# Loads of the stored projection weights begun from ScalarE's queue instead of SyncE's

## The chip, the cores and the metric

One core of one Trainium2 chip runs the whole program. The metric is the device time of one execution in microseconds (us). The core's engines each have an instruction stream of their own, run in order: TensorE (PE, with its weight loads as PEld), VectorE (DVE), ScalarE (ACT), GpSimd (POOL) and SyncE (SP). A transfer between HBM and on-chip memory is begun by an instruction in the stream of one of them; 16 DMA engines then move it.

## The reference

One inference step of a backbone with one layer: 128 context tokens and 2,048 latent tokens of width 1,024. Cut to what matters here:

```
h    = rmsnorm(x) * (1 + scale) + shift              # per token
proj = h @ w_in                                      # 1,024 -> 3,088 columns
u, z_s5, qkv, z_gdn, beta, a = split(proj)
s5   = gelu(S5 scans of u, both directions) * sigmoid(z_s5)
gdn  = gated DeltaNet of silu(conv3(qkv)), both directions, gated by silu(z_gdn)
x    = x + gate * (concat(s5, gdn) @ w_out)
x    = x + gate * (relu(rmsnorm(x)... @ w_mlp_in)^2 @ w_mlp_out)
out  = rmsnorm(x), and the final S5 and DeltaNet states of the context
```

Matrix products are made in three passes, since each float32 operand is split into a high and a low part: high by high, low by high, high by low.

## The kernel before

**Stages.** Time in the program falls into three stretches. Up to about 410 us the kernel normalises the tokens, makes tables, and projects the first group of tokens. From 410 to about 1424 us it projects the other groups, and beside that runs the S5 scans (lines 1265 to 1375), the DeltaNet preparation (lines 587 to 829) and the DeltaNet steps (lines 869 to 990). From 1424 us on it makes the output projection and the MLP (lines 1448, 1534 and 1556).

**The projection.** `group_proj` (line 471) walks over column tiles `ct` of 128 columns of `w_in`. For each it gets two weight tiles of 128 x 8 x 128 floats (512 KB each), the high part `wh` and the low part `wl`, and runs 24 matmuls a block of tokens on line 482: eight with `wh` on the high part of the tokens `hH`, eight with `wl` on `hH`, eight with `wh` on the low part `hL`. The sums stand in a PSUM bank `d`, of which there are three and, in the later groups, two. `evac` (line 490) empties the bank: for the qkv columns ScalarE (line 502), VectorE (504, 506), ScalarE (508), VectorE (510), then a store from SyncE (514); for the z columns lines 495 to 498 and 517 to 521.

**The weights.** The first time a column tile is needed, `load_w` (line 392) loads it raw, splits it and stores both parts in HBM in `s_wc` (line 398); 20 tiles are stored so. Each later time it loads the two stored parts back (line 403). This happens 68 times, so there are 136 such loads, 71 MB in all. The pool `pw` has two buffers for `wh` and two for `wl`: a load can begin when the last matmul that reads the tile of two column tiles before has run.

**What sets the order.** The program is written as generators that take turns, and a scheduler then puts the instructions of every engine into one fixed order by a timeline of its own. Each DMA raises one of eight completion semaphores, DMAHW0 to DMAHW7, that are given out in turn; before a DMA begins, its engine waits until the DMA that held the same semaphore before has landed. In the kernel before all DMAs of the program are begun by SyncE, so a load on line 403 stands in one stream with the stores of lines 514, 521, 720 and 756 and with the other loads, among them the tokens `hH` and `hL` (line 387).

Of the kernel before, what the change touches and what calls it, by code (L numbers as in the profile page):

```python
# [8 lines left out]
F32 = mybir.dt.float32  # L9
# [382 lines left out]
def load_w(k, ct):  # L392

    nc = k.nc
    if ct not in k.wdone:
        wh, wl = split_w(k, k.I['w_in'][0][:, ct * 128:ct * 128 + 128])
        for i, w in enumerate((wh, wl)):
            nc.sync.dma_start(k.S['wc'][ct, i], w.bitcast(F32).rearrange("p k c->p (k c)"))
        k.wdone.add(ct)
        return wh, wl  # L400
    ws = [k.pw.tile([128, 8, 128], FR, name=n) for n in ("wh", "wl")]
    for i, w in enumerate(ws):
        nc.sync.dma_start(w.bitcast(F32).rearrange("p k c->p (k c)"), k.S['wc'][ct, i])
    return ws


def split_w(k, src, p=None, nm=""):
    nc = k.nc
    p = p or k.pw
    wh = p.tile([128, 8, 128], FR, name="wh" + nm)  # L410
    wl = p.tile([128, 8, 128], FR, name="wl" + nm, bufs=1 if nm else k.wlb)
    w = k.pwr.tile([128, 8, 128], F32, name="wraw")
    nc.sync.dma_start(w, src.rearrange("(k p) c->p k c", p=128))
    nc.scalar.activation(wh, w, AF.Copy)
    nc.gpsimd.tensor_tensor(wl, w, wh.bitcast(F32), op=OP.subtract)
    return wh, wl
# [54 lines left out]
def group_proj(k, gi, cts):  # L471
    nc, I = k.nc, k.I
    H, L, blocks, off = k.cur
    for ct in cts:
        wh, wl = load_w(k, ct)
        for (f, w, span, segs) in blocks:
            ps = k.psd.tile([128, 512], F32, name="d")
            n = 0

            for (W_, X_) in ((wh, H), (wl, H), (wh, L)):  # L480
                for kk in range(8):
                    nc.tensor.matmul(ps[:, 0:w], W_[:, kk, :], X_[kk][:, f:f + w], start=(n == 0), stop=(n == 23))  # L482
                    n += 1
            evac(k, ct, ps, span, segs, off)
        if ct == 23:
            k.zg |= {c for (f, w, span, segs) in blocks for (o, m, tk) in segs for c in range(tk // 128, (tk + m + 127) // 128)}
        yield None
# [1420 lines left out]
```

## Time and profile before

| | |
|---|---|
| Three timed runs | 3278.9, 3288.34, 3278.14 us; median 3278.9 us |
| The profiled execution | 3283.95 us, its span 3282.2 us |
| Busy in the span | PE 3018.0, PEld 2554.5, DVE 1986.4, ACT 1113.0, POOL 1351.0 us |
| Mean granted TensorE clock | 0.946 |
| DMA | 594.98 MB, mean 181 GB/s |

A busy time is the time in which an engine had at least one instruction at work; the rest of the span it waited for another engine, for a transfer or for nothing that the profile shows. Instructions that begin a DMA are not counted as busy. They are marked with a q behind the engine's name (SPq). The granted clock is the share of TensorE's full speed: 1.0 stands for 2.4 GHz, 0.5 for 1.2 GHz.

### The profile page before, as it was taken

To read this page: it belongs to the slowest core of one execution; us is meant where nothing else is said; L and a number is where in the kernel's file an instruction comes from. 1 tells how busy PE (TensorE), PEld (TensorE's weight loads), DVE (VectorE), ACT (ScalarE), POOL (GpSimd) and SP (SyncE) were. 2 spreads that over 40 slices of the span, in tenths; PEclk is the share of its full clock that TensorE was granted. 3 is DMA by queue.
4 is the path that set the end of the run, shared out by engine and by line. 5 is a ranking of instruction groups with operands and counts; after the bars stand their busy time and mean duration, and the time that the engine had idled before them with its cause. 6 is when DMAs were issued, how large, how long until landed. Compare 5 with 4: busy or idle time off the path is not lost. (4 is left out here: it accounts for less than half of the span.)

```text
span 3282.2 us, 48952 instructions
## 1 busy us (share of the span) xinstructions
PE 3018.0 (92%) x17978; PEld 2554.5 (78%) x17978; DVE 1986.4 (61%) x3842; ACT 1113.0 (34%) x2338; POOL 1351.0 (41%) x983
## 2 busy tenths in 40 slices
PE   5899989889887889988999999999999999999998
PEld 2778967677776677877888778898888887888886
DVE  6635579777776886346545368543358643684445
ACT  2334334424433222234423243322233322433332
POOL 3532223413444332246543454333444544554542
PEclk7889989898988899989999999999999999999999
DMA  7789888966567888899533455322444534553332
GB/s 208 174 178 223 237 292 259 303 220 205 176 223 228 259 277 287 299 301 321 163 95 112 150 164 167 103 77 75 134 123 143 156 97 125 164 170 100 97 96 71
DMA packets 572752, 594.98 MB, mean 181 GB/s; under 512 B 167228, under 2 KB 428592, under 8 KB 569440
## 3 DMA queue, kind: packets, MB, share of 16 engines
q1 hardware_dynamic: 572512, 591.86, 58.9%
q8 instruction: 141, 2.31, 0.3%
q14 instruction: 99, 0.81, 0.1%
HBM read 449.61 MB, written 142.13 MB: 180 GB/s over the span
## 5 line engine op out<-in xcount | busy, mean ns | idle before, releaser
L1411 POOL TENSOR_TENSOR wol<-woraw,woh 128x512 fp32r<-128x512 f32 x320 | 426.7, 1345 | 648.4 <-ACT woh L1410 637.2
L1410 ACT ACTIVATE woh<-woraw 128x512 fp32r<-128x512 f32 x320 | 193.4, 626 | 802.8 <-PE gA L1556 470.8
L1561 DVE TENSOR_TENSOR acc<-acc,gA 128x512 f32<-128x512 f32 x510 | 341.0, 682 | 192.5 <-PE gA L1556 192.4
L1556 PE MATMUL gA<-woh,ffH 128*128 128x512 f32 x1088 | 426.0, 392 | 6.8 <-ACT r L1538 3.9
L1556 PE MATMUL gA<-woh,ffL 128*128 128x512 f32 x1088 | 425.5, 391 | 1.8 <-DVE ffL L1542 1.8
L1556 PE MATMUL gA<-wol,ffH 128*128 128x512 f32 x1088 | 425.0, 391 | 0.0
L1411 POOL TENSOR_TENSOR wil<-wiraw,wih 128x1024 fp32r<-128x1024 f32 x128 | 328.6, 2569 | 112.0 <-PE gA L1534 84.7
L1541 DVE TENSOR_TENSOR r<-r 128x512 f32<-128x512 f32 (+1 forms) x160 | 163.9, 1031 | 304.7 <-ACT ffH L1540 304.4
L1534 PE MATMUL gA<-htH,wih 128*128 128x512 f32 (+1 forms) x1280 | 276.6, 362 | 5.8 <-DVE acc L1561 3.3
L1534 PE MATMUL gA<-htL,wih 128*128 128x512 f32 (+1 forms) x1280 | 272.8, 358 | 0.0
L1534 PE MATMUL gA<-htH,wil 128*128 128x512 f32 (+1 forms) x1280 | 271.9, 357 | 0.0
L1534 PEld LDWEIGHTS gA<-htH,wih 128*128 128x128 f32 x1280 | 222.8, 190 | 39.1 <-DVE acc L1561 5.0
L1534 PEld LDWEIGHTS gA<-htL,wih 128*128 128x128 f32 x1280 | 221.5, 188 | 30.6
L1556 PEld LDWEIGHTS gA<-woh,ffH 128*128 128x128 f32 x1088 | 205.4, 189 | 51.2 <-ACT r L1538 4.8
L1534 PEld LDWEIGHTS gA<-htH,wil 128*128 128x128 f32 x1280 | 220.5, 188 | 29.8
L1556 PEld LDWEIGHTS gA<-woh,ffL 128*128 128x128 f32 x1088 | 205.3, 189 | 44.0 <-DVE ffL L1542 2.2
L1556 PEld LDWEIGHTS gA<-wol,ffH 128*128 128x128 f32 x1088 | 205.3, 189 | 43.0
L482 PE MATMUL d<-hH,wh 128*128 128x258 f32 (+2 forms) x960 | 178.8, 329 | 23.1 <-DMA wh<-s_wc 18.2
L482 PE MATMUL d<-hL,wh 128*128 128x258 f32 (+2 forms) x960 | 177.8, 319 | 9.5 <-DMA hL<-s_hL 9.4
L482 PEld LDWEIGHTS d<-hH,wh 128*128 128x128 f32 x960 | 150.8, 209 | 40.6 <-issue 24.2
L482 PE MATMUL d<-hH,wl 128*128 128x258 f32 (+2 forms) x960 | 176.0, 320 | 0.0
L1410 ACT ACTIVATE wih<-wiraw 128x1024 fp32r<-128x1024 f32 x128 | 134.7, 1052 | 121.1 <-PE gA L1534 80.7
(419 smaller groups left out, 5603.0 us busy)
## 6 DMA issues: line engine op xcount, KB each, us to landing
wiraw<-in_w_mlp_in SPq DMA_DIRECT2D x128, 512.0 KB
woraw<-in_w_mlp_out SPq DMA_DIRECT2D x256, 256.0 KB
wh<-s_wc SPq DMA_DIRECT2D x68, 512.0 KB
wl<-s_wc SPq DMA_DIRECT2D x68, 512.0 KB
wada<-in_w_ada SPq DMA_DIRECT2D x24, 1024.0 KB
KVr<-s_kv SPq DMA_DIRECT2D x34, 512.0 KB
Qr<-s_qkv SPq DMA_DIRECT2D x32, 512.0 KB
woraw<-in_w_out SPq DMA_DIRECT2D x64, 256.0 KB
```

What stands on the lines that cost most here:

```text
L482: nc.tensor.matmul(ps[:, 0:w], W_[:, kk, :], X_[kk][:, f:f + w], start=(n == 0), stop=(n == 23))
L1410: nc.scalar.activation(h[:, i:i + n], w, AF.Copy)
L1411: sub.tensor_tensor(l[:, i:i + n], w, h[:, i:i + n].bitcast(F32), op=OP.subtract)
L1534: nc.tensor.matmul(ps[b][:, 0:w], W[:, kk, :], X[:, kk, b * w:b * w + w], start=(m == 0), stop=(m == 23))
L1541: nc.vector.tensor_tensor(r[:, 0:w], r[:, 0:w], r[:, 0:w], op=OP.mult)
L1556: nc.tensor.matmul(ps, X[:, s], W[:, hf], start=(m == 0), stop=(m == 3 * FB - 1))
L1561: nc.vector.tensor_tensor(accs[i][:, c], accs[i][:, c], ps, op=OP.add)
```

## The change

One word in `load_w`: the two DMAs that load a stored column tile are begun from ScalarE's instruction stream.

```diff
@@ load_w, line 403
     ws = [k.pw.tile([128, 8, 128], FR, name=n) for n in ("wh", "wl")]
     for i, w in enumerate(ws):
-        nc.sync.dma_start(w.bitcast(F32).rearrange("p k c->p (k c)"), k.S['wc'][ct, i])
+        nc.scalar.dma_start(w.bitcast(F32).rearrange("p k c->p (k c)"), k.S['wc'][ct, i])
     return ws
```

The scheduler puts all streams into a new order. Without the waits, ScalarE's stream goes from 2,153 to 2,289 instructions and SyncE's from 1,956 to 1,820; TensorE's keeps its 15,585, of which the first 2,156 and the last 6,485 stand as before and those between are mixed differently. Two places follow, with the waits in brackets: a wait on an engine's name is for work of that engine, one on a DMAHW name for a transfer. The number behind a tile's name is that of its buffer.

SyncE before, around the loads of one column tile (`wh_8310`, `wl_8311`) in the second group of tokens; `s_qkv` and `s_rw` are stores to HBM of projected columns and of DeltaNet factors:

```order
L514 DMA s_qkv_70<-ec3_7956 128x2x128 [waits DMAHW2_49,DVE_49]
L756 DMA s_rw_73<-W_5966 4x16x1024 [waits DVE_49]
L756 DMA s_rw_73<-W_5966 4x16x1024
L514 DMA s_qkv_70<-ec3_7992 128x2x128 [waits DMAHW5_49,DVE_49]
L756 DMA s_rw_73<-UB_6312 4x16x1024 [waits DMAHW6_49,Activation_49]
L756 DMA s_rw_73<-UB_6312 4x16x1024 [waits DMAHW7_49]
L514 DMA s_qkv_70<-ec3_8082 128x2x128 [waits DMAHW0_49,DVE_49]
L403 DMA wh_8310<-s_wc_61 128x1024 [waits DMAHW1_49,PE_49]
L403 DMA wl_8311<-s_wc_61 128x1024 [waits DMAHW2_49]
```

ScalarE with the change, at the same loads; lines 502 and 508 are the evacuation of the blocks of the tile before, line 753 a DeltaNet copy:

```order
L403 DMA wh_8153<-s_wc_61 128x1024 [waits DMAHW5_49,DMAHW1_49]
L508 ACTIVATE ec2_7990<-ec1_7988 128x256 [waits DVE_49,Activation_49]
L502 ACTIVATE ec1_8074<-d_8049,cw_152 128x256 [waits PE_49,Activation_49]
L403 DMA wl_8311<-s_wc_61 128x1024 [waits DMAHW4_49,PE_49]
L508 ACTIVATE ec2_8080<-ec1_8078 128x256 [waits DVE_49,Activation_49]
L753 ACTIVATE UB_6312<-W_5966 128x1024 [waits DVE_49]
L502 ACTIVATE ec1_8110<-d_8085,cw_152 128x256 [waits PE_49,Activation_49]
L403 DMA wh_8310<-s_wc_61 128x1024 [waits DMAHW6_49,DMAHW3_49]
L508 ACTIVATE ec2_8116<-ec1_8114 128x256 [waits DVE_49,Activation_49]
```

The two loads have left the row of stores, and each now stands between two evacuations: `wl` ahead of the first step of a block's evacuation, `wh` behind it.

The second place is among the z columns, where DeltaNet steps (lines 934 and 955) run beside the projection. SyncE with the change, around the stores of the inverse (`s_inv`, line 829):

```order
L886 DMA Qr_13800<-s_qkv_70 128x1024 [waits DMAHW7_49,PE_49]
L829 DMA s_inv_76<-R0_12720 128x512 [waits DMAHW0_49,DVE_49]
L829 DMA s_inv_76<-R0_12720 128x512 [waits DMAHW1_49]
L829 DMA s_inv_76<-R1_12721 128x512 [waits DMAHW2_49,DVE_49]
L829 DMA s_inv_76<-R1_12721 128x512 [waits DMAHW3_49]
L887 DMA Rr_13802<-s_inv_76 128x512 [waits DMAHW4_49,PE_49]
L883 DMA KVr_13801<-s_kv_75 128x1024 [waits DMAHW5_49,PE_49,Pool_49]
```

and ScalarE with the change, at the load whose semaphore is DMAHW2, the same as that of the first store of `R1_12721` above:

```order
L955 ACTIVATE o_13749<-p4_13750,gsc_94 128x128 x3
L934 ACTIVATE w_13741<-p1_13736 128x512 [waits PE_49]
L403 DMA wl_14437<-s_wc_61 128x1024 [waits DMAHW2_49,DMAHW1_49,PE_49]
L517 ACTIVATE ec2_14297<-d_14272 128x512 [waits DVE_49,PE_49,Activation_49]
L403 DMA wh_14436<-s_wc_61 128x1024 [waits DMAHW6_49,DMAHW4_49]
L955 ACTIVATE o_13833<-p4_13834,gsc_94 128x128 [waits DMAHW6_49]
```

In the kernel before, the load `wl_14437` stood in SyncE's stream 22 DMAs ahead of the first of these stores; now the stores come first, and ScalarE waits for one of them to land before it begins the load and evacuates `d_14272`.

## Rows read from the trace of the kernel before

**Rows 1.** Stretches: busy us of PE, PEld, DVE, ACT, POOL; clock, DMA share, GB/s
```profile
410.00:1424.00 1014.00, 881.14 (x6971) 745.38 (x6968) 742.67 (x1925) 345.19 (x964) 333.17 (x298) 0.91 0.78 253
1424.00:3282.00 1858.00, 1791.76 (x8642) 1520.93 (x8640) 1017.43 (x1383) 616.74 (x1093) 870.64 (x553) 0.98 0.45 137
...
700.00:710.00 10.00, 2.90 (x13) 2.94 (x14) 5.86 (x28) 1.20 (x3) 0.71 (x2) 0.65 0.72 256
710.00:720.00 10.00, 10.00 (x94) 9.64 (x93) 5.46 (x19) 1.88 (x6) 2.42 (x2) 0.84 0.50 143
```

**Rows 2.** Line 403: its instructions (duration ns min/median/max, first and last start us)
```profile
L403 SPq DMA_DIRECT2D wh<-s_wc x68: 319/377/2693, 409.9 to 1414.5; - x68
L403 SPq DMA_DIRECT2D wl<-s_wc x68: 319/389/1875, 410.5 to 1412.3; - x68
```

**Rows 3.** What PE waited for, 410 to 1424 us (us in total, times, longest)
```profile
PE gs L1367 <- DVE S L1355: 23.3, 6, 7.3
PE d L482 <- DMA wh<-s_wc: 18.2, 10, 7.7
PE gT L660 <- ACT kv L650: 10.6, 3, 4.8
...
PE d L482 <- DMA hL<-s_hL: 9.4, 4, 7.5
...
PE g L786 <- DMA RW<-s_rw: 7.2, 1, 7.2
...
PE p L927 <- DMA Qr<-s_qkv: 4.6, 1, 4.6
PE p L937 <- ACT w L934: 4.2, 5, 1.3
```

**Rows 4.** What SP's queue waited for, 410 to 1424 us
```profile
SPq L403 <- PE d L482: 39.5, 34, 5.6
...
SPq L403 <- DMA hH<-s_hH: 2.3, 3, 1.2
```

**Rows 5.** SP in order of time, 688 to 710 us (start, duration)
```profile
690.88 2.08 SPq L514 DMA_DIRECT2D s_qkv<-ec  x1
693.06 2.95 SPq L756 DMA_DIRECT2D s_rw<-UB  x2
696.10 0.86 SPq L514 DMA_DIRECT2D s_qkv<-ec  x1
697.05 1.22 SPq L403 DMA_DIRECT2D wh<-s_wc  x1
```

**Rows 6.** PE in order of time, 688 to 712 us
```profile
689.89 1.11 PE L482 MATMUL d<-hL,wh 128*128 128x258 f32 x8
...
693.01 1.20 PE L482 MATMUL d<-hH,wh 128*128 128x258 f32 x8 [1.55 <-DMA wh<-s_wc]
...
707.10 3.78 PE L482 MATMUL d<-hH,wh 128*128 128x258 f32 x16 [7.71 <-DMA wh<-s_wc]
```

**Rows 7.** ACT in order of time, 676 to 710 us
```profile
692.15 0.46 ACT L502 ACTIVATE ec<-d,cw 128x256 f32<-128x256 f32 x1
```

**Rows 8.** What DVE waited for, 410 to 1424 us
```profile
DVE ga L1371 <- ACT ga L1370: 30.7, 15, 11.7
DVE ec L504 <- ACT ec L502: 22.5, 10, 4.5
DVE ec L496 <- ACT ec L495: 19.0, 8, 5.5
DVE R L803 <- ACT TA L802: 17.8, 9, 4.8
```

**Rows 9.** What ACT waited for, 410 to 1424 us
```profile
ACT U L740 <- DMA UB<-s_ub: 16.5, 4, 8.0
```

**Rows 10.** ACT in order of time, 1195 to 1203 us
```profile
1199.34 0.60 ACT L934 ACTIVATE w<-p 128x512 f32<-128x512 f32 x1 [4.16 <-PE p L932]
```

**Rows 11.** SP in order of time, 1194 to 1242 us
```profile
1235.32 2.08 SPq L829 DMA_DIRECT2D s_inv<-R  x4
```

## The prediction

> **What bounds the kernel now.** I read the stretches first. The loads that the change moves stand between 409.9 and 1414.5 us [rows 2], so the stretch from 410 to 1424 us is the one that it touches. There TensorE is busy 881.14 of 1014 us, VectorE 742.67, ScalarE 345.19, the DMA engines 0.78 of the time, and TensorE is granted 0.91 of its clock; behind it, TensorE is busy 1791.76 of 1858 us at 0.98 [rows 1]. The last stretch is TensorE's own work, which the change leaves as it is. The projection stretch has no single bound: TensorE lacks 1014 - 881 = 133 us in it, and only this idle time, and the clock that goes down behind it, can be won or lost.
>
> Next the waits of TensorE in that stretch. The longest entry, 23.3 us, is for VectorE in the S5 scan. The moved loads come second: matmuls waited 18.2 us in ten places for a `wh` tile, 7.7 of them in one. Other transfers, all begun by SyncE, cost 9.4 (`hL`), 7.2 (`RW`) and 4.6 us (`Qr`), together 21.2 [rows 3].
>
> Last, the orders of time around that longest wait. TensorE finished the last matmuls with an older `wh` at 689.89 + 1.11 = 691.00 us, and at 707.10 us it still waited for the tile that went into this buffer [rows 6]. SyncE had begun that load at 697.05 us only: from 690.88 us on it was at a store of line 514, two of line 756 and another of line 514 [rows 5]. The load was late because of what stood ahead of it in its stream, not only because of its transfer.
>
> **The change, part by part.** Sums are made against the profiled execution, 3283.95 us; its span is 3282.2 us, and the median of the three runs is 3278.9, 5.05 us less.
>
> *The loads' place.* In the new order the load at 697.05 us stands on ScalarE directly behind the line 502 that ended at 692.15 + 0.46 = 692.61 us [rows 7]. That is 4.44 us earlier, or 57% of the 7.71 us that TensorE waited. I take 57% of the 18.2 us: **-10.4 us**. The bounds are 0, if the transfers get no quicker by an earlier start, and -18.2.
>
> *The clock behind it.* In the 10 us with the wait TensorE was granted 0.65, in the next 0.84 [rows 1]: it had stood still, and then ran for a time at the lower level, 1.2 GHz, in place of 2.4. Sixteen matmuls then took 3.78 us where eight took 1.20 before [rows 6], so 1.4 us were lost on these. I take **-2 us** for all ten places; bounds 0 and -4.
>
> *SyncE's stream.* It loses 68 x 0.377 + 68 x 0.389 = 52.1 us of issuing [rows 2] and 39.5 us of waiting for TensorE to leave a buffer [rows 4], 91.6 us or 9% of the stretch. What stands behind can start earlier by some of that. The other loads that TensorE waited for are worth 21.2 us; 9% of it is **-2 us**, bounds 0 and -21.2.
>
> *ScalarE's stream.* It gains the 136 issues, 52.1 us if each takes there what it took on SyncE; the trace of before shows no DMA begun by ScalarE, so the bounds are 0 and 52.1. ScalarE is busy a third of the stretch, but it is waited for: VectorE's four largest waits for it make 90.0 us [rows 8], TensorE's two largest 14.8 us [rows 3], 10.3% of the stretch. A delay of ScalarE counts about there: 10.3% of 52.1 is 5.4 us if all these waits are on the path, 1.5% of it, 0.8 us, if TensorE's alone are. I take **+3 us**. What is queued behind an issue is line 508 or line 502 of the same column tile, in the first place shown; line 508 waits for two steps of VectorE anyhow. The loads pass no instruction on POOL's queue.
>
> *ScalarE's new waits.* A load waits for TensorE to leave the buffer, and for one or two completion semaphores (two or more in 87 of the 136). The first is cheap: the evacuation behind it waits for nearly the same matmuls. The second no row shows on ScalarE. Nearest is the same load on SyncE, which waited 2.3 us in three places for `hH` to land, 0.77 each [rows 4]; farther is ScalarE's wait for `UB`, 16.5 us in four places, 4.1 each [rows 9]. If one load in five (27) holds ScalarE for 4.1 us, that is 111 us, of which 10.3% is 11 us. Between 0 and +11 I take **+3 us**, nearer to the load's own row.
>
> *The new mixture.* Everything between 410 and 1424 us is reordered. This has no sign that I can read; a tenth of the 133 us of idle time is 13 us, which I take as its bound on either side.
>
> The sum is -10.4 - 2 - 2 + 3 + 3 = -8.4 us: 3275.6 us against the profiled execution, 3270.5 on the scale of the median, **3271 us**. A measurement of this kernel can tell about 0.3% from no change, 9.8 us, so this is no measurable change, though close to a gain.
>
> **The Trainium skill against this.** The row shows a load held up behind other issues for 6 us [rows 5]. The Trainium skill, "DMA: Bandwidth & Descriptors", section "Issuing engines are not separate DMA queues", says that transfers begun by several engines run on the same 16 DMA engines and interleave, and that only the sequencer's time to begin them is saved, usually little beside the transfer. By that rule the first and third term would be about nothing. The trace differs at that place: the time in SyncE's stream ahead of the load, 6 us, is not little beside the 10 us from its issue to the end of the wait.
>
> **The rivals.**
>
> *The transfer is what counts.* From the issue at 697.05 to the end of the wait at 707.10 us went 10 us; a load that begins earlier may only meet other traffic, and the queue it is begun from decides nothing. Then the first three terms fall away and +6 stays: 3285 us. For it: a DMA share of 0.78 over the stretch [rows 1]. Against it: in the 10 us of the longest wait the share was 0.72, below that mean. Chance 0.15, also without measurable change.
>
> *Faster: SyncE was the knot.* If the loads are on time and SyncE's other loads too, all of 18.2 + 21.2 + 4 us goes, less 6: -37 us, 3242. Two thirds of the 43 us, less the 6, are more likely: -22 us, about 3257 us. For it: SyncE began loads of three kinds that TensorE waited for. Against it: much of TensorE's idle time is for VectorE, which would be late next. Chance 0.34.
>
> *Slower: ScalarE held by the stores of SyncE.* In the second place shown, the load on DMAHW2 must wait until the store of the inverse has landed. In the trace ScalarE was through with line 934 at 1199.34 + 0.60 = 1199.94 us [rows 10], and the stores of line 829 began at 1235.32 us [rows 11], since VectorE had not made their tiles before. If they come as late again, ScalarE stands for over 35 us, with the evacuation of `d_14272` behind it; TensorE goes on until its two banks are full, and SyncE meets the same when the semaphore it wants is held by a load that ScalarE has not begun. At half its length one such hold costs 18 us and turns the sum into +10 us, the edge of what can be told; two give 3307 us. Between them I take 3298 us. It decides from 18 us that reach TensorE. Against it: the scheduler has put VectorE's work for these tiles earlier too. Chance 0.29.
>
> **How the numbers follow.** The sum itself has 0.22, within 0.3%; with the first rival "same" has 0.37, faster 0.34, slower 0.29. The likeliest case's own range is the band from 3269 to 3289. For 8 times in 10 the range reaches to 3248 us, past the half gain by the bounds of the first term, and to 3304 us, nearly to two holds: about one tenth is left on either side.
>
> **What would show it.** Right: in the new profile the wait of line 482 for `wh` shrinks from 18.2 us to about 8, the 136 issues stand under ACT's queue at about 0.38 us each, ACT's queue waits for landings with a few us in all, and the stretch ends near 1416 us. Wrong towards slower: ACT's queue waits tens of us for `s_inv`, `s_ub` or `s_rw`, and PE for lines 502 and 517. Wrong towards faster: the waits for `hL`, `RW` and `Qr` go as well, and the clock in the stretch rises above 0.91. A change behind 1424 us would be none of these terms.

## The result, and the profile after

The change made the kernel slower: 3329.26 us in the median of 4 runs (3318.8 to 3338.07) against 3283.04 us for the kernel before on the same chip (4 runs, 3278.14 to 3288.34). The ratio is 1.0139, 95% interval 1.0102 to 1.0176, or +46 us. That lies outside the forecast range. The profiled execution took 3326.23 us, its span 3324.4, 42.2 us more than before.

The loads now end later. Line 403 of the changed kernel (duration ns min/median/max, first and last start us), which answers to [rows 2]:

```profile
L403 ACTq EVENT_SEMAPHORE  x119: 17/17/16795, 399.9 to 1466.4; - x119
L403 ACTq DMA_DIRECT2D wl<-s_wc x68: 326/326/353, 400.1 to 1468.2; - x68
L403 ACTq DMA_DIRECT2D wh<-s_wc x68: 326/326/389, 401.4 to 1470.8; - x68
```

An issue costs ScalarE 0.326 us, less than SyncE's 0.377 and 0.389, and nearly always the same. But the last load begins at 1470.8 us, 56 us later than before, and one wait in front of a load took 16.8 us.

The stretches, cut at the last load. The columns are those of [rows 1]. The kernel before:

```profile
410.00:1415.00 1005.00, 872.14 (x6917) 736.38 (x6914) 739.71 (x1920) 341.77 (x951) 330.61 (x295) 0.91 0.78 254
1415.00:3282.00 1867.00, 1800.76 (x8696) 1529.93 (x8694) 1020.39 (x1389) 620.15 (x1107) 873.21 (x555) 0.98 0.45 137
```

The changed kernel:

```profile
410.00:1471.00 1061.00, 893.80 (x6897) 752.73 (x6898) 741.42 (x1919) 341.61 (x946) 332.11 (x295) 0.88 0.74 239
1471.00:3324.00 1853.00, 1789.59 (x8728) 1524.17 (x8727) 1011.10 (x1397) 623.81 (x1120) 875.22 (x556) 0.99 0.45 139
```

The whole loss is made in the first of them. TensorE's idle time there grew from 1005 - 872 = 133 to 1061 - 894 = 167 us (+34), and its busy time by 22 us for as many matmuls, at a granted clock of 0.88 in place of 0.91. Behind it 14 us came back, so 42 us are left in the span.

What TensorE waited for, 405 to 1480 us (us in total, times, longest), to be held against [rows 3]:

```profile
PE p L937 <- ACT w L934: 19.8, 7, 7.9
PE gs L1367 <- DVE S L1355: 19.2, 9, 7.6
PE gT L620 <- DVE ngc L618: 14.3, 3, 7.3
PE gs L1294 <- ACT S L1298: 14.2, 2, 8.5
...
PE d L482 <- DMA wh<-s_wc: 9.6, 5, 5.1
...
PE d L482 <- DMA hL<-s_hL: 2.1, 2, 1.7
```

The wait for `wh` is halved, from 18.2 to 9.6 us, and that for `hL` nearly gone. In their place TensorE waits for ScalarE: 19.8 us for `w` of the DeltaNet step, which was 4.2, and 14.2 us for line 1298, which was 1.3. Added up over the same 405 to 1480 us by what ended them, TensorE's waits for transfers fell from 43 to 21 us, while those for ScalarE rose from 31 to 55 and those for VectorE from 70 to 93.

What ScalarE waited for, same stretch. The first answers to [rows 9]; the others have no counterpart in the kernel before:

```profile
ACT U L740 <- DMA UB<-s_ub: 25.4, 4, 15.5
...
ACT G L789 <- DMA hH<-s_hH: 16.6, 1, 16.6
...
ACT w L934 <- DMA wl<-s_wc: 12.6, 1, 12.6
...
ACT S L1298 <- DMA s_pk<-PK: 11.7, 1, 11.7
...
ACT ec L508 <- DMA hL<-s_hL: 9.2, 1, 9.2
ACT ec L502 <- DMA hH<-s_hH: 8.0, 1, 8.0
```

Evacuations and DeltaNet steps that need no `hH`, `hL` or `s_pk` now stand behind these transfers, because a load ahead in their stream waits for them. The longest is seen in order of time. ScalarE:

```profile
1217.76 0.60 ACT L934 ACTIVATE w<-p 128x512 f32<-128x512 f32 x1 [0.46 <-PE p L932]
1234.62 0.33 ACTq L403 DMA_DIRECT2D wl<-s_wc  x1
1234.99 0.38 ACT L789 ACTIVATE G<-g 128x256 f32<-128x256 f32 x1 [16.63 <-DMA hH<-s_hH]
```

and TensorE beside it:

```profile
1228.82 2.10 PE L482 MATMUL d<-hL,wh 128*128 128x512 f32 x8
1235.43 0.25 PE L797 MATMUL g<-G,RW 32*32 32x32 f32 x1 [4.51 <-ACT G L789]
```

ScalarE was through at 1218.36 us and began the `wl` load at 1234.62, 16.26 us later. Line 789 stood behind it, and TensorE stopped for 4.51 us. So of a stand of 16 us some 4.5 reached TensorE.

I added up such gaps over all 136 loads of the trace (from the end of ScalarE's instruction before a load to the load's begin): **191 us**. In 115 us of it the event that came last was the landing of an earlier transfer, in 74 us TensorE's leaving the buffer. In the kernel before, SyncE stood 62 us before the same loads, 14 for landings and 48 for TensorE. I call this time *standing* below. Only part of it reaches TensorE. Of TensorE's 55 us of waiting for ScalarE, five waits with 33.8 us together are waits during which such a stand ended; the 4.51 us above are one of them.

### The profile page after: what moved, and what is told of

Read it like the earlier page. It is cut to its first block, busy times and chain, and to the rows that moved or that the text cites. A ratio compares the mean times of both kernels' runs of the same rounds, so it can differ in the third digit from the quotient of the medians.

```text
span 3324.4 us, 48939 instructions
## 1 busy us (share of the span) xinstructions
PE 3026.9 (91%) x17978; PEld 2565.2 (77%) x17978; DVE 1975.8 (59%) x3842; ACT 1112.7 (33%) x2338; POOL 1355.5 (41%) x983
## 4 chain that ended last, share of the span: by engine, by line
PE 59%; DVE 16%; DMA 14%; issue 4%; SPq 2%; POOL 2%; ACT 2%; ACTq 0%; DVEq 0%; POOLq 0%
PE gA L1534 19%; PE gA L1556 19%; PE d L482 7%; PE gA L1448 3%; PE d L307 2%; DVE S L1349 1%; DMA s_qkv<-ec 1%; PE gs L1367 1%; PE gs L1294 1%; DMA woraw<-in_w_out 1%; DVE Tt L1312 1%; DVE W L749 1%; DVE UB L747 1%; DVE S L1314 1%; POOL wol L1411 1%
## 5 line engine op out<-in xcount | busy, mean ns | idle before, releaser
L1541 DVE TENSOR_TENSOR r<-r 128x512 f32<-128x512 f32 (+1 forms) x160 | 174.4, 1097 | 310.4 <-ACT ffH L1540 310.3
L482 PE MATMUL d<-hH,wh 128*128 128x258 f32 (+2 forms) x960 | 188.5, 340 | 29.2 <-DVE ec L506 11.2
L482 PEld LDWEIGHTS d<-hH,wh 128*128 128x128 f32 x960 | 158.4, 219 | 47.7 <-issue 32.1
```

Source lines behind the costliest of these rows:

```text
L1541: nc.vector.tensor_tensor(r[:, 0:w], r[:, 0:w], r[:, 0:w], op=OP.mult)
```

## The experiments

Every ratio is that to the kernel before on the same chip, with its 95% interval. The theories, as they came up: **S**, ScalarE stands behind landings (**P**: behind full buffers); **B**, the 136 issues take 136 x 0.326 = 44 us of ScalarE; **M**, the scheduler's new order costs it, whatever the queue.

### Parts of the change

The loads of the z columns alone (64), of the qkv columns alone (72), of `wh` alone and of `wl` alone (68 each):

```diff
-        nc.sync.dma_start(w.bitcast(F32)...
+        (nc.scalar if ct in ZCOLS else nc.sync).dma_start(w.bitcast(F32)...      # e1
+        (nc.scalar if ct not in ZCOLS else nc.sync).dma_start(w.bitcast(F32)...  # e2
+        (nc.scalar if i == 0 else nc.sync).dma_start(w.bitcast(F32)...           # e5
+        (nc.scalar if i == 1 else nc.sync).dma_start(w.bitcast(F32)...           # e6
```

> Only the 64 loads for the z columns (from about 1000 us on) are begun by ScalarE, the 72 for the qkv columns by SyncE as before. Theory S (ScalarE stands at a load until a transfer that SyncE begins has landed, since both draw on the same eight completion semaphores): the longest holds in the changed kernel's trace lie behind 1050 us, so most of the +46 us comes from these: +25 to +40 us. Theory B (the time ScalarE takes to begin the loads, 136 x 0.326 us): 64 of 136, +22 us. Theory M (the new order of the stretch costs time by itself): only what stands behind the 5,440th matmul moves, +10 to +25 us. None: within 10 us of before.

> Only the 72 loads for the qkv columns (410 to about 1000 us) are begun by ScalarE. S: shorter holds of ScalarE here, +5 to +20 us. B: 72 of 136, +24 us. M: the order differs from the 2,156th matmul on as in the changed kernel, so nearly the whole +46 us.

> Only the 68 wh loads are begun by ScalarE, the wl loads by SyncE. In the changed kernel's trace ScalarE stands before its 136 loads for 115 us that end with a landing (45 before wh, 70 before wl) and 74 us that end with TensorE leaving the buffer (2 before wh, 73 before wl: wl is free in the middle of a block, wh at its end, when the evacuation behind it can begin too). Theory S, only landings cost: +18 us. Theory P, only standing for the buffer costs: within 5 us of before. Theory H, any standing of ScalarE costs alike, 47 of 191 us: +11 us.

> Only the 68 wl loads are begun by ScalarE. S: +28 us. P: +45 us, the whole. H, 143 of 191 us: +35 us.

| loads from ScalarE | us | ratio |
|---|---|---|
| z columns (e1) | 3304.41 | 1.0062 [1.0043, 1.0081] |
| qkv columns (e2) | 3306.89 | 1.0065 [1.0041, 1.0089] |
| `wh` (e5) | 3306.97 | 1.0073 [1.0051, 1.0094] |
| `wl` (e6) | 3317.04 | 1.0104 [1.0081, 1.0127] |

A loss in us is here and below the ratio's, unless the medians are named. Each half costs 20 to 34 us. Split by columns the halves add up to 42 us, near the whole; split by `wh` and `wl` they add up to 58. No part carries the loss alone. ScalarE stood some 108 us before the loads of e1 and 47 us before those of e2, and yet the two cost the same, so the length of the standing doesn't set the loss by itself. The scheduler wrote a new order each time, so these runs don't separate the theories.

### The issue time by itself

The loads stay with SyncE, and ScalarE gets short copies behind its evacuations (the trace has 136 of them of 0.27 us, 37 us in all):

```diff
-            evac(k, ct, ps, span, segs, off)
+            evac(k, ct, ps, span, segs, off); [nc.scalar.activation(k.junk, ps[:, 0:128], AF.Copy) for _ in range((2 if len(blocks) == 1 else 1) if k.again else 0)]
```

> All loads stay with SyncE. ScalarE gets 140 more instructions of about 0.31 us beside the evacuations, which copy a part of the bank d into a tile that nothing reads; the order of TensorE's work changes about as much as with the change itself (10,021 of 15,585 matmuls keep their place; 10,229 with the change). S: no hold at a transfer, so within 10 us of before. B: the whole loss, +35 to +50 us. M: +20 to +50 us. A ScalarE wait for a landing in the trace stays as before.

3289.21 us, 1.0012 [0.9998, 1.0026]. **B falls as the whole of the loss**: nearly as much time on ScalarE (37 us, where the issues take 44) costs 4 us by the ratio, 2 by the medians and at most 9 by the interval. The order was a new one here too, and what it costs or gains by itself isn't known.

### Another queue

```diff
-        nc.sync.dma_start(w.bitcast(F32)...
+        nc.gpsimd.dma_start(w.bitcast(F32)...
```

> All 136 loads are begun by GpSimd, whose transfers have eight completion semaphores of their own: ScalarE and SyncE get no wait for them, GpSimd waits for TensorE to leave the buffer. S: ScalarE is not held, so at most +10 us; the wait of the projection for wh goes below 18 us. B: no issue on ScalarE, same as before. M: the order changes more than with the change (9,707 keep their place): +20 to +50 us. A theory P, that an engine with other work which waits for the buffer is what costs, says +20 us or more, with GpSimd's other work late.

3337.77 us, 1.0152 [1.0127, 1.0177]: POOL is no better a place. What it stood for (405 to 1480 us):

```profile
POOL wl L403 <- PE d L482: 165.2, 39, 14.0
...
POOL wh L403 <- PE d L482: 59.8, 30, 9.5
```

An engine that also computes stands for the buffers here, 225 us of it. S and B, which left no more than 10 us, miss; P and M don't. Its order is again one of its own.

### The same change under other orders

`wh` and `wl` loaded as one tile by one DMA (e7 from ScalarE, e8 from SyncE), and the S5 scans advanced at another rate than 2, which changes the mixture (1.9: e9 SyncE, e10 ScalarE; 2.1: e11 SyncE, e12 ScalarE):

```diff
+    nc.scalar.dma_start(w2.bitcast(F32)..., k.S['wc'][ct].rearrange("i p c->p i c"))   # e7; e8: nc.sync
```

```diff
-            scans = Side(2, [s5_part(k, hb) for hb in range(8)])
+            scans = Side(1.9, [s5_part(k, hb) for hb in range(8)])   # e9, e10; e11, e12: 2.1
```

> wh and wl of a column tile share one tile and are loaded with one transfer of 1 MB, begun by ScalarE: 68 loads, each free only when the last matmul of a column tile has run. To be set against the same with SyncE (next run). S: half the landings waited for, some 55 us, +20 us. P: the buffer is free when the evacuation can begin, so nothing, within 8 us. H: 55 of 191 us, +13 us.

> The same joint loads begun by SyncE: 68 issues fewer on SyncE and 68 fewer completion semaphores drawn, but the low part comes later than before. By all theories within 15 us of before; under it if SyncE's stream and the semaphores are what projection lacks, over it if the later low part is.

> SyncE begins the loads as before. One number of the program is changed, the rate at which the S5 scans are written between the projection's column tiles (1.9 steps a tile in place of 2): the same instructions in another order, 10,157 of 15,585 matmuls in their old place. Theory M (any new order of the stretch costs, since the order of before is a good one among many): +15 to +35 us, as with the joint loads from SyncE. Theories S, P and H (the loss is in ScalarE's stream): within 8 us of before.

> The same rate of 1.9, loads begun by ScalarE. M: as far above before as the run with SyncE at this rate, within 10 us. S, P, H: 35 to 50 us above that run.

> SyncE begins the loads; the scans' rate is 2.1 (10,729 matmuls in their old place). M: +15 to +35 us. S, P, H: within 8 us of before.

> Rate 2.1, loads begun by ScalarE. M: within 10 us of the run with SyncE at this rate. S, P, H: 35 to 50 us above that run.

| | SyncE: us, ratio | ScalarE: us, ratio | difference, us |
|---|---|---|---|
| as given | 3283.04 | 3329.26, 1.0139 | +46 |
| rate 1.9 | 3305.90, 1.0058 [1.0039, 1.0078] | 3303.84, 1.0062 [1.0036, 1.0089] | -2 |
| rate 2.1 | 3289.32, 1.0025 [1.0002, 1.0047] | 3324.04, 1.0108 [1.0078, 1.0139] | +35 |
| one joint load | 3312.28, 1.0088 [1.0064, 1.0112] | 3296.88, 1.0044 [1.0024, 1.0064] | -15 |

The differences are those of the medians; by the ratios they are +1, +27 and -14 us in the last three rows, each uncertain by some 10 to 12 us. The same change of queue is thus worth anything from -15 to +46 us. e10 came as M had it and e12 nearer to S, P and H; e7 and e8 missed what every theory expected. A small change of rate by itself, loads on SyncE, cost 19 us in one case and 8 in the other by their ratios, so an order alone can cost nearly half as much as the change did. In e10 ScalarE stood 164 us before its loads, nearly as long as in the changed kernel, and nothing was lost against e9. What differs is what TensorE needed from behind the loads: its waits during which such a stand ended are two with 9.1 us in e10 and five with 26.8 us in e12, against five with 33.8 in the changed kernel.

### Queue and order apart

Now the order was held still. The loads are numbered as the program asks for them, and a set of numbers says which of them ScalarE begins:

```diff
-        nc.sync.dma_start(w.bitcast(F32)...
+        k.nl = getattr(k, 'nl', -1) + 1; (nc.scalar if k.nl in MOVED else nc.sync).dma_start(w.bitcast(F32)...
```

For e13 the set has 90 loads with which every other instruction, on all five engines, keeps its place in the order of the kernel before. For e14 it has the 49 loads that are left when as many as possible go back to SyncE with every other instruction in the order of the changed kernel.

> 90 of the 136 loads of L403 come from ScalarE's queue, chosen so that the order of everything else on every engine is that of the kernel before; 46 stay with SyncE. Theory Q (the queue itself: ScalarE stands behind a landing or a full buffer in its own order) expects 90/136 of the 46 us: +30 us, a ratio of about 1.009, with the PE waits for ScalarE (p behind w, d behind ec) longer than before. Theory M (the loss is in the other order that the scheduler wrote when the loads changed engine) expects no change: ratio 0.997 to 1.003. A ratio of 1.004 to 1.006 says that each has a half.

> The order of everything else on every engine is that of the changed kernel; 87 of the 136 loads go back to SyncE's queue, 49 stay on ScalarE's. Theory Q expects 49/136 of the 46 us: +17 us, a ratio of about 1.005. Theory M expects the loss of the changed kernel to stay: ratio 1.010 to 1.017, although ScalarE stands before a third of the loads only.

| | us | ratio | ScalarE stood |
|---|---|---|---|
| e13: old order, 90 loads from ScalarE | 3305.54 | 1.0064 [1.0044, 1.0085] | 125 us |
| e14: new order, 49 loads from ScalarE | 3327.33 | 1.0133 [1.0114, 1.0153] | 82 us |
| the changed kernel: new order, 136 | 3329.26 | 1.0139 [1.0102, 1.0176] | 191 us |

With the order of before, the queue alone costs 21 us for 90 of the 136 loads: its part is shown. With the order of after, taking 87 loads and 109 us of standing away from ScalarE gives back some 2 us, within the intervals, as M had it. That looks as if the rest belonged to the order, and the waits have to show whether it does. e14 (405 to 1480 us):

```profile
POOL S L924 <- DVE S L943: 183.2, 15, 18.0
...
DVE S L943 <- PE p L937: 41.8, 15, 11.8
...
PE p L937 <- ACT w L934: 21.4, 8, 8.2
...
PE gs L1294 <- ACT S L1298: 15.7, 2, 9.2
```

The changed kernel has 174.2, 39.4, 19.8 and 14.2 us in these four rows. e13:

```profile
POOL S L924 <- DVE S L943: 94.6, 11, 16.3
...
DVE S L943 <- PE p L937: 19.6, 8, 8.6
...
PE p L937 <- ACT w L934: 9.8, 5, 4.9
...
PE gs L1294 <- ACT S L1298: 1.1, 1, 1.1
```

The kernel before has 98.2, 14.5, 4.2 and 1.3. So the waits of the DeltaNet step (lines 924 to 943) and of line 1294 stay when two thirds of the loads have left ScalarE. But the largest of them stand behind loads that ScalarE still begins in e14. One is seen in order of time there, ScalarE first:

```profile
1054.58 0.42 ACT L495 ACTIVATE ec<-d 128x256 f32<-128x256 f32 x1
1065.57 0.33 ACTq L403 DMA_DIRECT2D wh<-s_wc  x1
1065.94 0.69 ACT L1298 ACTIVATE S<-gs 128x272 f32<-128x272 f32 x2 [10.94 <-DMA s_pk<-PK]
```

and TensorE:

```profile
1066.39 1.17 PE L1294 MATMUL gs<-ub,WI 128*64 128x272 f32 x4 [9.22 <-ACT S L1298]
```

ScalarE stood for 10.57 us before this load, and TensorE waited 9.22 us for the line behind it. TensorE's waits during which such a stand ended are five with 33.8 us in the changed kernel, four at the same places with 32.0 us in e14, and three with 21.2 us in e13. By this count the 87 loads that went back had held TensorE up for 1.8 us only, and that nothing came back without them doesn't show that the order by itself costs anything.

What the new order costs beside the standing isn't told apart. At e13's price of 21/125 = 0.17 us for each us of standing, an estimate, e14's 82 us are worth 14 of its 43 us, which leaves 29 for the order; by TensorE's waits, also an estimate, they are worth 32, which leaves 11. That something beside the standing costs time in a new order is seen in e1, e2, e5 and e6: such waits are 6 to 13 us there, the losses 20 to 34. e14's 49 loads couldn't be moved back without a new order, so the new order with all loads on SyncE wasn't tried.

### What of the queue costs

The 90 loads of e13 were split by whether ScalarE had stood for more than 1 us before them there: 31 had (120 of the 125 us), 59 had not. The edit is that of e13 with the smaller sets, the order that of before.

> The order of before again, on every engine. Of the 90 loads of e13 only those 31 come from ScalarE before which it stood for more than 1 us there (120 of its 125 us). Theory H (the queue's cost is ScalarE's standing) expects nearly all of the 21 us that e13 cost: +14 to +21 us, a ratio of 1.004 to 1.0065. Theory N (each load costs its share, by its issue or by crossing the work of ScalarE) expects 31/90 of it: +7 us, 1.002.

> The order of before, and the other 59 of the 90 loads from ScalarE, before which it stood for 5 us in all. Theory H expects no change: ratio 0.9985 to 1.0015, and few new stands of ScalarE. Theory N expects 59/90 of 21 us: +14 us, 1.004. A sum of e15 and e16 that is far from e13's 1.0064 would say that the two parts aren't independent.

| | us | ratio | ScalarE stood | last load begins |
|---|---|---|---|---|
| e15: the 31 held loads | 3302.01 | 1.0053 [1.0032, 1.0073] | 118 us | 1440.6 us |
| e16: the 59 free loads | 3298.08 | 1.0031 [1.0015, 1.0047] | 29 us | 1419.1 us |

The 31 loads cost 17 us, nearly as much as all 90, as H expected. The 59 cost 10 [5 to 15 by the interval], where standing as known from e13 would have made it 0: H misses here, and N's 14 is inside the interval. Once the others are gone, new stands come up before these too (the longest 10.3 us). The two ratios add up to 1.0084, above e13's 1.0064 but inside the intervals. For each load the cost is 17/31 = 0.55 against 10/59 = 0.17 us, so the loads with standing cost more. TensorE's waits during which a stand ended are two with 16.0 us in e15 and two with 9.3 us in e16, near the two losses, so standing can account for both. At e13's price the 29 us of e16 would be worth only 5 of the 10, and whether the 59 cost anything beyond their standing stays open. A third buffer for the tiles, which would shorten the wait for TensorE, wasn't tried.

The stretches can't be set against each other in the same way. The profiled execution of e15 took 3313.02 us, 11 more than its median, and that of e16 3288.74, 9 less than its own, so they lie 24 us apart where the medians lie 4 apart. e15, to its last load:

```profile
410.00:1441.00 1031.00, 899.68 (x6924) 756.39 (x6925) 741.37 (x1922) 342.55 (x956) 329.61 (x296) 0.88 0.76 248
```

e16:

```profile
410.00:1419.00 1009.00, 872.71 (x6921) 737.15 (x6922) 744.34 (x1924) 343.86 (x955) 330.07 (x296) 0.90 0.78 253
```

In this execution of e15 TensorE is idle for 131 us, no more than before, but works at a clock of 0.88 and is busy 28 us longer for as many matmuls; this one of e16 is near the kernel before in both. Over the whole program the clock was 0.937 in this execution of e15, and 0.944 to 0.946 in nine of its twelve, which is what the kernel before has (0.940 to 0.950 beside them): the low clock isn't what e15 costs in the median.

## Why the prediction was wrong

**The loads' place: the number came, its cause isn't shown.** The forecast was a `wh` wait of about 8 us; it is 9.6, so 8.6 of the 10.4 us were won at that row. In the first place shown, the loads went out between the evacuations as the order had them. But in e3, with SyncE's loads in another order, the same wait is 12.8 us; in e13, with the order of before, it is 19.1, of which 5.9 are for loads from ScalarE and 13.3 for those left with SyncE. So the rival in which only the transfer counts isn't settled by it.

**The clock: wrong in sign.** It was to rise a little with shorter waits for `wh`. It fell from 0.91 to 0.88 in the stretch, and TensorE's busy time there grew by 22 us. TensorE also stood still for 34 us more, but in the profiled e15 the clock is 0.88 without more idle time, so what made it fall isn't shown.

**SyncE's stream: right in kind, no gain in time.** The wait for `hL` went from 9.4 to 2.1 us, that for `RW` stayed (7.2 and 7.7). But SyncE didn't run ahead: what is now its longest wait, for VectorE before the stores of line 514, went from 30.2 to 58.0 us. The next late engine was VectorE.

**ScalarE's stream: not contradicted.** The 136 issues were priced at +3 us; e3 measured +4 [-1 to +9 by the interval] for nearly as much time, in an order of its own.

**ScalarE's new waits: the first step that failed.** The prediction said that a wait for TensorE to leave the buffer "is cheap", took landings from "one load in five (27)" at 4.1 us, 111 us at most, and settled on +3 us between 0 and +11, "nearer to the load's own row". The standing was 191 us, 74 of it for the buffer that was called cheap, and the waits of TensorE during which a stand ended make 33.8 us. The prediction had a row for the buffer: it credited SyncE with the 39.5 us that it would no longer wait there [rows 4], and charged ScalarE with nothing for the same waits. SyncE's 0.77 us a wait was the wrong neighbour, perhaps because there the load stood behind instructions that waited for the same things first; that isn't shown. With the order kept, the queue cost +21 us [+14 to +28 by the interval] for 90 of the 136 loads.

**The new mixture: the second, a bound too narrow.** It had "no sign that I can read", with 13 us as its bound on either side. e9, in which the order alone is changed, lost 19 us [13 to 26 by the interval], and the pairs show that the same change of queue may come out with either sign: -15, -2, +35 and +46 us, a spread of 61 us. The term had no sign, as said; its bound was too small, and the upper end of the range with it. How much of the +46 is the new order's own isn't shown: 11 or 29 us by the two estimates from e14.

**The rival "Slower: ScalarE held by the stores of SyncE"** had the right kind of cause, with 0.29. Its place was right in part: before `wl_14437` ScalarE stood for 9.3 us, until TensorE had left the buffer; the stores of `s_inv`, begun at 1250.61 us, had landed by then. Instead of one hold of 35 us there were some 40 of over 1 us. Its "18 us that reach TensorE" were passed, with 33.8; TensorE waited for lines 934 and 1298, not for the 502 and 517 that were named as the sign.

So of the +46 us, whose own interval is 33 to 58, between 46 - 29 = 17 and some 33 us (0.17 x 191 = 32, or the 33.8 of TensorE's waits) are the queue, by its standing. The other 13 to 29 are left for the order that the scheduler wrote. All of these are estimates, and how the two share what lies between wasn't settled. e3 and e11, the fastest of the other kernels, are not faster than the kernel before.

The Trainium skill, "DMA: Bandwidth & Descriptors", "Issuing engines are not separate DMA queues", had spoken against a gain, and none came. It says that only the sequencer's time is saved, and the runs don't settle that: the wait for `wh` fell by 8.6 us, but by 5.4 in e3 too, where SyncE began the loads. The part of the loss that is shown came from elsewhere: from what the engine that begins the transfer can't do while it waits.

## What to carry to other kernels

Before a DMA is moved to an engine that computes, list every event that it waits for, its completion semaphore and its buffer too, and ask for each how late it is against the engine's next instruction: that standing is paid by all that is queued behind. Then ask what the busiest engine needs from there: 125 us of standing cost 21 in e13, and 164 us cost nothing against e9 in e10. Where a scheduler rewrites the order, a single before-and-after comparison mixes the edit with a re-sort that can be worth as much; hold the order still by moving only what leaves it unchanged, or repeat the edit under several orders.

## What was not expected of the hardware

Beginning the same 512 KB load took 0.326 us on ScalarE with hardly any spread in the changed kernel (326 to 389 ns; single ones took up to 1.47 us in e12), 0.32 to 2.69 us on SyncE, and 0.53 to 0.76 us on POOL in e4. The median from a load's begin to its landing, read load by load, was about 5.8 us from SyncE and 4.8 us from ScalarE. The loads thus landed sooner after their begin in the kernel that got slower. And beside 34 us more of idle time, 22 us more of busy time went with a clock of 0.88 in place of 0.91: idle time alone would have understated the loss of the stretch.
